# State products interleaved with the gate products, and adaLN sums moved forward and onto VectorE, in a two-layer trunk

## The chip, the core and the metric

One NeuronCore of a Trainium2 chip runs the whole program. The metric is the device time of one execution in microseconds. The kernel before has a median of 759.27 us over 3 runs (758.9 to 759.5).

## The reference, cut to what matters

The trunk has two layers for 256 tokens of width 1024. Layer 0 mixes tokens by gated linear attention (GLA), layer 1 by a recurrent block (RG-LRU); each is followed by a mixture of 16 experts of which every token uses 2. Shifts, scales and gates of all of them ("adaLN vectors") come from one conditioning vector `c` and large matrices `ada_w`. All arithmetic is float32.

```python
cond = silu(c)
for i in range(2):
    sh1, sc1, g1, sh2, sc2, g2 = split(cond @ ada_w[i] + ada_b[i], 6)
    h = rmsnorm(x, norm_mix_g[i]) * (1 + sc1) + sh1
    x = x + g1 * (gla_mixer(h, ...) if i == 0 else lru_mixer(h, ...))
    h = rmsnorm(x, norm_ffn_g[i]) * (1 + sc2) + sh2
    x = x + g2 * grouped_moe(h, ...)
return rmsnorm(x, final_norm_g)
```

In the GLA mixer four chunks of 64 tokens follow each other: the state of a chunk is `S_n = diag(gamma_n) S_{n-1} + k_dec^T v`, for four heads of 128 x 256 each, and its output is `o_n = q_n^T S_n`, normed and multiplied by `silu(g)`; then comes `w_out`.

## The kernel before

**The stream.** Every large weight comes in pieces of 128 x 2048 float32 (1 MB), issued by SyncE in one order that `plan` writes down as a text (lines 285 to 287). `a10` is layer 0's adaLN vector 1, half 0 (two pieces); `A..` the same of layer 1; `i4` two pieces of the mixer's input matrix, `I2` and `J2` one half of one each; `o` the output matrix (four pieces); `u0` to `u6` the units of the expert block. u0 holds the experts 0 and 1 at fixed places, 12 pieces; u1 to u6 hold the others in an order that is known only after the routing (`r_ordi`, line 951, read by SyncE at line 242). The pieces lie in a ring of 17 slots, which also holds the mixer's large tiles (`big`: v, the states S, sg, oT, xg). A piece is issued when a slot is free.

**The adaLN vectors.** `jobs` lists them in the order of the stream. `fill` (line 303) sums one half of a vector on VectorE: one scaling and seven multiply-adds of 128 x 512 (lines 319 and 317), at a low priority, so that they stand where VectorE would otherwise be idle; a gate ("wide") gets a ninth operation (line 321). The others sum into one of two buffers `acc`. `settle` (line 343) finishes what `fill` left: a matmul with ones for a gate (line 349), four transposes (line 353), a reduction (line 356) and one or two small operations for the others. `fill_now` (line 325) does the same sum on TensorE with 16 matmuls (line 338) and a copy by ScalarE.

**The order of work.** The program is written with a scheduler: it orders each engine's instructions by their place in the program (or their priority) and by when it thinks their inputs are ready, and gives out slots and buffers. Only in the output projection (`out_route`, line 463) is TensorE's order that of the text.

**Layer 0's mixer** (`gla`, line 533). The k, v and gate projections use I2, I3, I1, J2, J3, J1; the q projection (line 613) i0. The constants of layer 1's mixer (`lru_consts`, line 704) are worked out in between, in some 25 operations of 128 x 8 on VectorE. The states follow for both tiles of 128 tokens: 16 products per tile (line 629), which VectorE copies into S or adds to the state before (lines 637 and 639). Then the g projection in two halves (i4 and i5, line 529), the outputs `o_part` (line 655), their gating (line 666) and the transposes `turn` (line 674).

**Layer 0's output and routing** (`out_route`). Four parts of `w_out` (line 473), by tile m and half hf, each followed by two VectorE operations that add to x (lines 475 and 476). Between their matmuls stand the transposes of x, the router's products (line 830) and the settlements. `scores` (lines 834 and 835: `r_z`, then a sigmoid on ScalarE), `choose` (lines 843 to 863) and `route_count` pick the experts of one tile; behind the second tile's, `route_order` (lines 941 to 951) sorts the experts by load and writes `r_ordi`. A10 and A11 are filled behind the first tile's `choose`; A00 and A01 are `fill_now`, one ahead of tile 1's routing and one behind its `choose`. What is owed then (a50, a51, A10, A11, A00, A01) is settled in the expert block, between u0's up products (line 1030) and its down products (line 1041).

Of the kernel before, what the change touches and what calls it, by code (L numbers as in the profile page):

```python
# [10 lines left out]
OP = mybir.AluOpType  # L11
# [3 lines left out]
P = 128  # L15
D = 1024
S = 256
NM = S // P
# [57 lines left out]
def trunk(ctx, tc, I, out):  # L76
# [16 lines left out]
    def mid(name):  # L93
        return wk.tile([P, 1024], F32, name="mid", tag="mid", bufs=3)
# [171 lines left out]
    def plan(l, text):  # L266

        for n in text.split():
            if n[0] == "a":
                stream.add("a", *ada_pieces(l, int(n[1]), int(n[2])))  # L270
            elif n[0] == "A":
                stream.add("a", *ada_pieces(1, int(n[1]), int(n[2])))
            elif n[0] == "i":
                w = (gw_in, lw_in)[l]
                stream.add("i", k_piece(w, 0, int(n[1]) * 512), k_piece(w, 1, int(n[1]) * 512))
            elif n[0] in "IJ":
                stream.add("i", k_piece((gw_in, lw_in)[l], "IJ".index(n[0]), int(n[1]) * 512))
            elif n == "r":
                stream.add("r", gate_piece(I["lru_w_r"][0]), gate_piece(I["lru_w_i"][0]))
            elif n == "o":  # L280
                stream.add("o", *[row_piece(I[("gla_w_out", "lru_w_out")[l]][0], q) for q in range(4)])
            else:
                stream.add("u", *moe_pieces(l, UNITS[int(n[1])]))

    plan(0, "a10 a00 I2 a11 I3 a01 I1 J2 J3 J1 i0 a20 a21 i4 a40 a41 i5 a30 a31 a50 a51 o A10 A11 A00 A01 "
            "u0 u1 u2 u3 u4 u5 u6")
    plan(1, "i2 i3 a20 r i0 a21 a40 i1 a41 a30 a31 o a50 a51 u0 u1 u2 u3 u4 u5 u6")

# [51 lines left out]
        A.copy(acc, ps)  # L340
        owed.append((acc, dst[:, 4 * hf:4 * hf + 4], r, gain + hf if gain is not None else None, True))

    def settle(n=99):

        for _ in range(min(n, len(owed))):
            acc, dst, r, gain, four = owed.pop(0)
            ps = bank()
            if dst is None:
                T.matmul(ps, ones, acc, start=True, stop=True)
                A.copy(acc, ps)  # L350
                continue
            for j in range(4):
                T.transpose(ps[:, j * P:(j + 1) * P], acc.rearrange("r (p j) -> r j p", j=4)[:, j, :], ident)

            rows_of = ps.rearrange("p (j q r) -> p j q r", j=4, q=4)[:, :, :, 0] if four else ps.rearrange("p (j q) -> p j q", j=4)
            V.tensor_reduce(dst, rows_of, axis=AX.X, op=OP.add)
            if gain is None:
                V.tensor_tensor(dst, dst, tabT[:, :, r], op=OP.add)
            else:
                V.scalar_tensor_tensor(dst, dst, 1.0, tabT[:, :, r], op0=OP.add, op1=OP.add)  # L360
                V.tensor_mul(dst, dst, tabT[:, :, gain])
# [98 lines left out]
    def out_route(l, yT, gate, gs, rest=None, last=None):  # L460

        w = [stream.get("o").rearrange("p (j n) -> p j n", j=2) for _ in range(4)]
        stream.look = SLOTS - 2
        h, hT = new_h()
        R = route_begin()

        def part(m, hf, between={}):
            sl = slice(hf * 512, (hf + 1) * 512)
            ps = bank()
            for k in range(8):  # L470
                if k in between:
                    between[k]()
                T.matmul(ps, yT[:, k, m * P:(m + 1) * P], w[k // 2][:, k % 2, sl], start=k == 0, stop=k == 7)  # L473
            tmp = s2("tmp")
            V.tensor_mul(tmp, ps, gate[:, sl])
            b = V.tensor_add(x[:, m, sl], x[:, m, sl], tmp)
            mark["x"] = b.ins

        def first():
            turn_h(x, hT, 0, halves=[1])  # L480
            stats_of[0] = stats(0)
            scaled(h, 0, stats_of[0])

        late = len(jobs) > 2
        stats_of = [None, None]
        with tc.manual_schedule(engines={T.engine}):
            part(0, 0)
            part(0, 1, {3: lambda: turn_h(x, hT, 0, halves=[0])})
            if rest:
                rest()  # L490
            router(R, gs)
            part(1, 0, {2: lambda: settle(2), 4: first, 6: lambda: router_shift(R, gs[1], 0), 7: lambda: logits(R, hT, 0)})
            router_shift(R, gs[1], 1)
            scores(R, 0, stats_of[0])
            choose(R, 0)
            fill(2)
            part(1, 1, {3: lambda: turn_h(x, hT, 1, halves=[0]), 5: lambda: logits(R, hT, 1, halves=[0]),
                        7: lambda: route_count(R, 0)})
            stream.ahead(stream.at + SLOTS - 1)
            r = stats(1)  # L500
            if late:
                accs = mid("acc")
                fill_now(accs[:, 0:512])
            else:
                settle(1)
            turn_h(x, hT, 1, halves=[1])
            xg, oh = gather_begin(R)
            gather_tile(R, h, oh, 0, 0, [0])
            logits(R, hT, 1, halves=[1])
            scores(R, 1, r)  # L510
            scaled(h, 1, r)
            gather_tile(R, h, oh, 0, 0, [1, 2, 3])
            choose(R, 1)
            gather_tile(R, h, oh, 0, 1)
            route_count(R, 1)
            if late:
                fill_now(accs[:, 512:1024])
            else:
                settle(1)
            if last:  # L520
                last()
            gather_end(l, R, h, xg, gs)
        R["xg"] = xg
        return h, hT, R
# [11 lines left out]
    def gla(gs):  # L536
# [40 lines left out]
            T.matmul(ps[32 * q:32 * q + 32, 0:S], wa[:, k, :], hT[:, k, :], start=k < 4, stop=k >= 4)  # L577
        V.tensor_scalar(alr, ps[:, 0:S], e16, None, op0=OP.add)
        half_proj(0, 1)
        for m in range(NM):  # L580
            A.copy(v[:, m, 0:512], pst[0][m])

# [5 lines left out]
        for m in range(NM):  # L588
            A.activation(ed[:, m], ed[:, m], AF.Ln, bias=1.0)
            V.scalar_tensor_tensor(la[:, m], psz[m], 0.0, ed[:, m], op0=OP.min, op1=OP.subtract)  # L590
        half_proj(1, 1)
        for m in range(NM):
            A.copy(v[:, m, 512:1024], pst[1][m])
        half_proj(2, 1)
        psg = bank()
        for m in range(NM):
            ps = bank()
# [12 lines left out]
        for hd in range(4):  # L610
# [1 line left out]
            for k in range(8):  # L612
                T.matmul(ps[:, 0:S], w[k // 4][:, k % 4, hd * P:(hd + 1) * P], hT[:, k, :], start=k == 0, stop=k == 7)
            A.activation(qT[:, hd], ps[:, 0:S], AF.Copy, scale=128.0 ** -0.5)
        fill(2)
        k0.extend(lru_consts())


        Sb = [big("S").rearrange("p (c n) -> p c n", c=2) for _ in range(2)]
        St = [Sb[c // 2][:, c % 2].rearrange("p (h n) -> p h n", h=4) for c in range(4)]  # L620

        for m in range(NM):
            for h2 in range(2):
                pair = [bank(), bank()]
                for hh in range(2):
                    hd = 2 * h2 + hh
                    for c in range(2):
                        rows_of = slice(64 * c, 64 * c + 64)
                        T.matmul(pair[c][:, hh * 256:(hh + 1) * 256], kd[rows_of, m, hd * P:(hd + 1) * P],
                                 v[rows_of, m, hd * 256:(hd + 1) * 256], start=True, stop=True)  # L630
                for c in range(2):
                    k = 2 * m + c
                    for hh in range(2):
                        hd = 2 * h2 + hh
                        src = pair[c][:, hh * 256:(hh + 1) * 256]
                        if k == 0:
                            V.tensor_copy(St[k][:, hd], src)  # L637
                        else:
                            V.scalar_tensor_tensor(St[k][:, hd], St[k - 1][:, hd], gam[:, hd * 4 + k:hd * 4 + k + 1],
                                                   src, op0=OP.mult, op1=OP.add)  # L640
        sg = big("sg").rearrange("p (m n) -> p m n", m=2)

        def g_part(hf, m, w):
# [26 lines left out]
        def turn(m, hf):  # L670
# [4 lines left out]
            for b in range(2):  # L675
# [4 lines left out]
                else:  # L680
                    V.tensor_scalar(dst, src, ngT[:, b:b + 1], None, op0=OP.mult)

        w = get2()
        for m in range(NM):
            g_part(0, m, w)
        fill(2)
        os = [o_part(m) for m in range(NM)]
        for m in range(NM):
            gated(m, 0, *os[m])
        settle(2)  # L690
        w = get2()
        g_part(1, 0, w)
        gated(0, 1, *os[0])
# [2 lines left out]
            turn(m, 0)  # L696
        g_part(1, 1, w)
        gated(1, 1, *os[1])
        fill(4)
        settle(2)  # L700
        turn(0, 1)
        return oT[0], lambda: turn(1, 1)

# [108 lines left out]
    def router_shift(R, s, at):  # L812

        ps = R["ps"][:, 3 * NE:4 * NE]
        if at == 0:
            R["b"] = sm.tile([1, NE], F32, name="r_b", bufs=1)
            for k in range(8):
                T.matmul(ps[0:1], s[:, k:k + 1], rw[:, k, :], start=k == 0, stop=k == 7)
            V.tensor_copy(R["b"], ps[0:1])
        else:  # L820
            R["bb"] = rt("bb", NE)
            T.matmul(ps, ones[0:1, :], R["b"], start=True, stop=True)
            V.tensor_copy(R["bb"], ps)
# [425 lines left out]
```

## Time and profile before

| | us |
|---|---|
| median of 3 runs | 759.27 |
| the profiled execution | 757.96 |
| its span, first to last instruction | 756.2 |
| TensorE busy | 699.6 |
| VectorE busy | 340.4 |
| ScalarE busy | 131.4 |
| weights and others moved by DMA | 286.27 MB, 379 GB/s on average |

The page divides the span into 40 slices of 18.9 us. Windows and timelines give stretches in microseconds from the span's start; "PEclk" is the TensorE clock that was granted (1.00 is full speed), "DMA share" the mean busy share of the 16 DMA engines. In a timeline, instructions of one line that follow each other are one row: start, time from the first's start to the last's end, engine, line, operation, operands, count, and in brackets the idle time before it with what ended it. SPq is the queue in which SyncE issues DMAs.

### The profile page before, as it was taken

How to read it: one execution, taken by the hardware profiler on the slowest of the kernel's cores; microseconds unless marked ns; L12 is line 12 of the kernel's file. 1: busy time of each engine (PE TensorE's matmuls, PEld its weight loads, DVE VectorE, ACT ScalarE, POOL GpSimd, SP SyncE). 2: the span in 40 equal slices, each digit the busy share in tenths (PEclk: the TensorE clock that was granted, in tenths of full speed). 3: DMA queues.
4: the chain of work that ended last, by engine and by line, in shares of the span. 5: the costliest groups of instructions: out<-in, count | busy, mean ns of one | idle time of the engine just before them, and what ended most of it. 6: DMA issues, size and time to landing. Idle time of an engine off the chain costs nothing. (4 is left out here: it accounts for less than half of the span.)

```text
span 756.2 us, 9538 instructions
## 1 busy us (share of the span) xinstructions
PE 699.6 (93%) x3559; PEld 342.8 (45%) x3559; DVE 340.4 (45%) x780; ACT 131.4 (17%) x257; POOL 27.4 (4%) x69
## 2 busy tenths in 40 slices
PE   4899899999999999999887999998999999999874
PEld 3345745454633533533226888655433433433212
DVE  3626983897413223231023589996523143140214
ACT  5006112122200000000013166123210010010002
POOL 5000001000000000000000014000000000000000
PEclk9999999999999999999999999999999999999998
DMA  9999999779999999999999999991999999999994
GB/s 304 384 386 387 386 396 386 269 318 384 423 370 422 421 421 420 423 409 422 411 363 379 381 367 350 406 377 59 423 421 419 419 421 421 421 420 410 422 373 150
DMA packets 80445, 286.27 MB, mean 379 GB/s; under 512 B 5991, under 2 KB 16280, under 8 KB 57866
## 3 DMA queue, kind: packets, MB, share of 16 engines
q1 hardware_dynamic: 78752, 284.71, 96.0%
q10 hardware_dynamic: 1258, 0.66, 0.3%
q8 instruction: 30, 0.49, 0.3%
q0 software_dynamic: 384, 0.23, 0.1%
q14 instruction: 21, 0.17, 0.1%
HBM read 284.54 MB, written 1.05 MB: 378 GB/s over the span
## 5 line engine op out<-in xcount | busy, mean ns | idle before, releaser
L1030 PE MATMUL ps<-w 128*32 128x512 f32 (+1 forms) x1280 | 204.1, 593 | 9.6 <-DMA w<-in_moe_w_up_dram 7.4
L1030 PEld LDWEIGHTS ps<-w 128*32 128x32 f32 (+1 forms) x1280 | 61.8, 121 | 148.7 <-issue 121.7
L1041 PE MATMUL ps<-w,s 128*32 128x512 f32 (+1 forms) x512 | 85.0, 594 | 2.7 <-ACT s L1160 2.7
L1147 DVE TENSOR_TENSOR s<-s,ps 128x512 f32<-128x512 f32 x14 | 9.6, 688 | 149.6 <-PE ps L1030 149.6
L1061 DVE TENSOR_TENSOR x<-x,ps 128x512 f32<-128x512 f32 (+1 forms) x60 | 39.1, 652 | 59.7 <-PE ps L1060 59.7
L317 DVE SCALAR_TENSOR_TENSOR acc<-w,cond,acc 128x512 f32<-128x512 f32 x84 | 64.8, 794 | 1.1
L473 PE MATMUL ps<-w 128*128 128x512 f32 x128 | 59.3, 599 | 0.0
L1060 PE MATMUL ps<-mid,s 128*128 128x512 f32 (+1 forms) x120 | 55.1, 581 | 2.9 <-DVE mid L1168 2.6
L740 PE MATMUL ps<-hT,w 128*128 128x256 f32 x256 | 55.7, 379 | 0.0
L1041 PEld LDWEIGHTS ps<-w,s 128*32 128x32 f32 (+1 forms) x512 | 25.6, 123 | 58.3 <-issue 50.9
L740 PEld LDWEIGHTS ps<-hT,w 128*128 128x128 f32 x256 | 48.7, 191 | 6.7 <-ACT hT L423 0.2
L1179 DVE TENSOR_TENSOR mid<-ps,gate 128x512 f32<-128x512 f32 x24 | 16.6, 692 | 64.7 <-PE ps L1041 64.7
L561 PE MATMUL ps<-w,hT 128*128 128x512 f32 x96 | 42.5, 596 | 1.8 <-DVE hT L425 1.0
L904 PE MATMUL ps<-onehot,h 128*128 128x256 f32 x192 | 42.4, 379 | 0.0
L317 DVE SCALAR_TENSOR_TENSOR gate<-w,cond,gate 128x512 f32<-128x512 f32 x56 | 40.9, 748 | 0.9
L1146 ACT ACTIVATE s<-ps 128x512 f32<-128x512 f32 x14 | 8.4, 597 | 183.6 <-PE ps L1030 183.6
L904 PEld LDWEIGHTS ps<-onehot,h 128*128 128x128 f32 x192 | 36.4, 190 | 7.0 <-issue 2.4
L1060 PEld LDWEIGHTS ps<-mid,s 128*128 128x128 f32 x120 | 20.5, 190 | 30.8 <-issue 20.1
L1160 ACT COPY s<-ps 128x512 f32<-128x512 f32 x14 | 8.2, 586 | 147.2 <-PE ps L1158 147.2
L529 PE MATMUL ps<-w,hT 128*128 128x512 f32 x64 | 29.6, 619 | 3.7 <-DVE w L637 3.7
L473 PEld LDWEIGHTS ps<-w 128*128 128x128 f32 x128 | 22.8, 191 | 20.7 <-issue 18.9
L561 PEld LDWEIGHTS ps<-w,hT 128*128 128x128 f32 x96 | 17.8, 190 | 23.9 <-issue 21.0
(261 smaller groups left out, 602.5 us busy)
## 6 DMA issues: line engine op xcount, KB each, us to landing
w<-in_moe_w_gate_dram SPq DMA_DIRECT2D x64, 1024.0 KB, 11.2
w<-in_moe_w_up_dram SPq DMA_DIRECT2D x64, 1024.0 KB, 15.7
w<-in_moe_w_down_dram SPq DMA_DIRECT2D x56, 1024.0 KB, 17.8
w<-in_ada_w_dram SPq DMA_DIRECT2D x48, 1024.0 KB, 13.5
w<-in_gla_w_in_dram SPq DMA_DIRECT2D x12, 1024.0 KB, 14.6
w<-in_moe_w_down_dram SPq DMA_DIRECT2D x16, 512.0 KB, 9.5
w<-in_lru_w_in_dram SPq DMA_DIRECT2D x8, 1024.0 KB, 12.5
w<-in_gla_w_out_dram SPq DMA_DIRECT2D x4, 1024.0 KB, 12.5
```

Source lines behind the costliest of these rows:

```text
L317: V.scalar_tensor_tensor(acc, w, cond[:, k:k + 1], acc, op0=OP.mult, op1=OP.add)
L473: T.matmul(ps, yT[:, k, m * P:(m + 1) * P], w[k // 2][:, k % 2, sl], start=k == 0, stop=k == 7)
L529: T.matmul(ps, hT[:, k, m * P:(m + 1) * P], w[k // 4][:, k % 4, :], start=k == 0, stop=k == 7)
L561: T.matmul(pst[i][m], hT[:, 4 * b + j, m * P:(m + 1) * P], w[:, j], start=b == 0 and j == 0, stop=b == 1 and j == 3)
L740: T.matmul(ps[:, 0:S], w[k // 4][:, k % 4, ct * P:(ct + 1) * P], hT[:, k, :], start=k == 0, stop=k == 7)
L904: T.matmul(ps[j // 2][:, j % 2 * 2 * P:(j % 2 + 1) * 2 * P], hv[:, b, j, :], oh, start=m == 0 and j % 2 == 0, stop=m == 1 and j % 2 == 1, ...
L1030: T.matmul(ps[p0:p0 + n], xg[:, k, t0 + p0:t0 + p0 + n], w[i][:, j, :], start=k == 0, stop=k == 7)
L1041: T.matmul(ps[hf][p0:p0 + n], aT[:, k, p0:p0 + n], w[i][:, j, hf * 512:(hf + 1) * 512], start=k == 0, stop=k == 3)
L1060: T.matmul(ps, wt[:, m * P:(m + 1) * P], y[:, sl], start=True, stop=True)
L1061: V.tensor_add(x[:, m, sl], x[:, m, sl], ps)
L1147: V.tensor_mul(act, act, pu)
L1179: V.tensor_mul(y[:, sl], py[hf], g2[:, sl])
```

## The change

The GLA's state products of a tile are followed at once by that tile's first g product, instead of all state products coming first. The adaLN pieces a20 to a41, a31, a50, a51, A10 and A11 stand nearer the front of the stream, and the calls of `fill` and `settle` move with them, from between the later parts of the mixer to between the earlier ones. In layer 0's output projection `fill_now` is gone: A00 and A01 are summed by `fill` like the others, behind the settlement of A10 and A11, whose buffers they use; a30 and a31 are settled in the mixer, a50 and a51 where `fill_now` stood. Functions that only change their place (`g_part`, `o_part`, `gated`, `turn`) are left out.

```diff
-    plan(0, "a10 a00 I2 a11 I3 a01 I1 J2 J3 J1 i0 a20 a21 i4 a40 a41 i5 a30 a31 a50 a51 o A10 A11 A00 A01 "
+    plan(0, "a10 a00 I2 a11 I3 a01 I1 J2 a20 J3 a21 J1 a40 i0 a41 a30 i4 a31 a50 a51 i5 A10 A11 o A00 A01 "
             "u0 u1 u2 u3 u4 u5 u6")
...
-    def settle(n=99):
-
-        for _ in range(min(n, len(owed))):
-            acc, dst, r, gain, four = owed.pop(0)
+    def settle(n=99, skip=0):
+
+        for _ in range(min(n, len(owed) - skip)):
+            acc, dst, r, gain, four = owed.pop(skip)
...
-        late = len(jobs) > 2
+        late = rest is not None
...
-            part(1, 0, {2: lambda: settle(2), 4: first, 6: lambda: router_shift(R, gs[1], 0), 7: lambda: logits(R, hT, 0)})
+            part(1, 0, {2: lambda: late or settle(2), 4: first, 6: lambda: router_shift(R, gs[1], 0), 7: lambda: logits(R, hT, 0)})
             router_shift(R, gs[1], 1)
             scores(R, 0, stats_of[0])
             choose(R, 0)
+            if late:
+                settle(2, 2)
             fill(2)
             part(1, 1, {3: lambda: turn_h(x, hT, 1, halves=[0]), 5: lambda: logits(R, hT, 1, halves=[0]),
                         7: lambda: route_count(R, 0)})
             stream.ahead(stream.at + SLOTS - 1)
             r = stats(1)
-            if late:
-                accs = mid("acc")
-                fill_now(accs[:, 0:512])
-            else:
-                settle(1)
+            settle(1)
             turn_h(x, hT, 1, halves=[1])
...
             route_count(R, 1)
-            if late:
-                fill_now(accs[:, 512:1024])
-            else:
-                settle(1)
+            settle(1)
...
         half_proj(0, 1)
+        fill()
...
         half_proj(1, 1)
+        fill()
...
         half_proj(2, 1)
+        fill()
...
-        fill(2)
+        fill()
+        settle(3)
+        fill()
         k0.extend(lru_consts())
...
-        for m in range(NM):
+        def states(m):
             for h2 in range(2):
                 pair = [bank(), bank()]
...
         w = get2()
         for m in range(NM):
+            states(m)
             g_part(0, m, w)
-        fill(2)
+        settle(1)
+        fill(3)
         os = [o_part(m) for m in range(NM)]
         for m in range(NM):
             gated(m, 0, *os[m])
-        settle(2)
         w = get2()
...
         g_part(1, 1, w)
         gated(1, 1, *os[1])
-        fill(4)
         settle(2)
+        fill(2)
         turn(0, 1)
```

## Rows read from the trace of the kernel before

**Rows 1.** The page's second part: DMA rate in 40 slices of the span.
```profile
GB/s 304 384 386 387 386 396 386 269 318 384 423 370 422 421 421 420 423 409 422 411 363 379 381 367 350 406 377 59 423 421 419 419 421 421 421 420 410 422 373 150
```
**Rows 2.** Windows, all engines: stretch, length, busy times, PEclk, DMA share, GB/s.
```profile
50.00:110.00 60.00, 56.28 (x196) 33.20 (x194) 45.54 (x93) 17.17 (x26) 0.00 (x0) 0.97 1.05 388
135.00:139.00 4.00, 4.00 (x11) 1.73 (x10) 4.00 (x7) 0.00 (x0) 0.00 (x0) 1.00 0.07 26
139.00:165.00 26.00, 25.92 (x112) 14.29 (x110) 23.07 (x53) 6.33 (x12) 0.56 (x1) 1.00 0.81 300
...
178.00:181.00 3.00, 3.00 (x21) 1.73 (x22) 1.89 (x6) 1.36 (x4) 0.00 (x0) 1.00 0.62 216
181.00:210.00 29.00, 28.32 (x134) 15.06 (x132) 14.08 (x53) 6.30 (x10) 0.00 (x0) 1.00 1.01 419
210.00:213.00 3.00, 3.00 (x16) 1.01 (x14) 0.02 (x1) 0.00 (x0) 0.00 (x0) 1.00 0.60 194
```
**Rows 3.** SyncE's own waits, 135 to 160 and 160 to 185: total, times, longest.
```profile
SPq L255 <- DVE acc L317: 14.8, 4, 8.8
...
SPq L242 <- DVE r_ordi L951: 10.1, 1, 10.1
```
**Rows 4.** Timeline of VectorE: `r_z` of tile 0 and `r_ordi`, layer 0.
```profile
158.94 0.23 DVE L834 SCALAR_TENSOR_TENSOR r_z<-ps,rstd,r_bb 128x16 f32<-128x16 f32 x1
...
177.41 0.16 DVE L951 CAST r_ordi<-r_ordf 1x14 int32<-1x14 f32 x1
```
**Rows 5.** Timeline of SyncE's DMA issues behind the order, layer 0 and layer 1.
```profile
178.61 1.56 SPq L255 DMA_DIRECT2D w<-in_moe_w_gate_dram  x2
...
210.38 4.38 SPq L255 DMA_DIRECT2D w<-in_moe_w_gate_dram  x4
...
527.42 2.69 SPq L255 DMA_DIRECT2D w<-in_moe_w_gate_dram  x4
...
555.74 4.34 SPq L255 DMA_DIRECT2D w<-in_moe_w_gate_dram  x4
```
**Rows 6.** Timeline of TensorE: q products, state products, g products.
```profile
73.37 14.00 PE L613 MATMUL ps<-hT,w 128*128 128x256 f32 x64
...
87.32 3.77 PE L629 MATMUL ps<-w,h 64*128 64x256 f32 x32
94.81 15.51 PE L529 MATMUL ps<-w,hT 128*128 128x512 f32 x32 [3.72 <-DVE w L637]
...
123.42 7.03 PE L529 MATMUL ps<-w,hT 128*128 128x512 f32 x16
```
**Rows 7.** Timeline of VectorE: the first states copied out.
```profile
94.01 0.75 DVE L637 COPY w<-ps 128x256 f32<-128x256 f32 x2
```
**Rows 8.** Window of TensorE behind the hole: busy, PEclk, DMA share, GB/s.
```profile
94.80:98.00 3.20, 3.19 (x4) 0.52 1.05 387
```
**Rows 9.** Windows of VectorE: two of all its work, then one of line 317 alone.
```profile
159.17:177.57 18.40, 16.09 (x68) 1.00 0.94 391
...
119.00:131.00 12.00, 1.70 (x5) 1.00 1.05 385
...
159.17:167.17 8.00, 5.71 (x8) 1.00 0.86 349
```
**Rows 10.** Timeline of VectorE: the first operation of a20.
```profile
55.89 0.49 DVE L319 TENSOR_SCALAR gate<-w,cond 128x512 f32<-128x512 f32 x1 [7.74 <-DMA w<-in_ada_w_dram]
```
**Rows 11.** Timeline of TensorE: the first `fill_now` of the projection, and settlements.
```profile
167.06 1.92 PE L338 MATMUL ps<-w,cond 128*32 128x512 f32 x16
...
194.85 1.88 PE L349 MATMUL ps<-gate,one 128*128 128x512 f32 x4
196.57 1.11 PE L353 MATMUL ps<-ident,acc 128*128 128x128 f32 x8
```
**Rows 12.** Timeline of VectorE: operations of the sums, and two settlements' reductions.
```profile
134.63 4.72 DVE L317 SCALAR_TENSOR_TENSOR acc<-w,cond,acc 128x512 f32<-128x512 f32 x7
...
150.49 1.28 DVE L356 TENSOR_REDUCE sh<-ps 128x4 f32<-128x512 f32 x2
```

More of the change, by code (lines that the diff above doesn't have):

```diff
@@ L620, in gla @@
         St = [Sb[c // 2][:, c % 2].rearrange("p (h n) -> p h n", h=4) for c in range(4)]
-        for m in range(NM):
[L623 to L640, printed above, removed]
         sg = big("sg").rearrange("p (m n) -> p m n", m=2)
@@ L681, in turn @@
                     V.tensor_scalar(dst, src, ngT[:, b:b + 1], None, op0=OP.mult)
+        def states(m):
+            for h2 in range(2):
+                pair = [bank(), bank()]
+                for hh in range(2):
+                    hd = 2 * h2 + hh
+                    for c in range(2):
+                        rows_of = slice(64 * c, 64 * c + 64)
+                        T.matmul(pair[c][:, hh * 256:(hh + 1) * 256], kd[rows_of, m, hd * P:(hd + 1) * P],
+                                 v[rows_of, m, hd * 256:(hd + 1) * 256], start=True, stop=True)
+                for c in range(2):
+                    k = 2 * m + c
+                    for hh in range(2):
+                        hd = 2 * h2 + hh
+                        src = pair[c][:, hh * 256:(hh + 1) * 256]
+                        if k == 0:
+                            V.tensor_copy(St[k][:, hd], src)
+                        else:
+                            V.scalar_tensor_tensor(St[k][:, hd], St[k - 1][:, hd], gam[:, hd * 4 + k:hd * 4 + k + 1],
+                                                   src, op0=OP.mult, op1=OP.add)
         w = get2()
         for m in range(NM):
+            states(m)
             g_part(0, m, w)
-        fill(2)
+        settle(1)
+        fill(3)
         os = [o_part(m) for m in range(NM)]
```

## The prediction

> **What bounds the kernel now.** I read the page's second part first: the DMA rate in 40 slices [rows 1]. It lies near 385 GB/s while layer 0's mixer runs, near 420 in the expert blocks, and falls off in slices 7 and 8 (132 to 170 us) and in slice 27. So the kernel streams weights, and what can be won lies in stretches where the stream stands still before the expert blocks. The windows split the first one [rows 2]: 7% DMA share from 135 to 139 us, 81% from 139 to 165, 62% from 178 to 181, 60% from 210 to 213; in between and after it is 1.01, full.
>
> Which of these gaps sets the end? SyncE's own waits answer [rows 3]. Up to 165 us it waits for ring slots that VectorE's adaLN sums still hold (8.8 us at the longest). Then it waits 10.1 us for `r_ordi`, the order of the routed experts, without which no further weight has an address. VectorE writes it at 177.41 to 177.57 us [rows 4], and the next issue is at 178.61 [rows 5]. At that point everything that may be loaded has been loaded: the share drops to 62%. So the gaps before 165 us cost nothing by themselves. Whatever is loaded sooner only waits longer for the order. The time of `r_ordi` is the one that the end follows, since the stream is full from there to the end of the block but for the gap at 210.
>
> What sets `r_ordi`? TensorE from 87 to 167 us with one hole: the 32 state products end near 91.1, then TensorE stands for 3.72 us for VectorE to copy a state out [rows 6], which starts at 94.01 behind the long chain of tiny `lru_consts` operations [rows 7]. For the first 3 us after the hole the granted clock is 0.52 [rows 8], near the lower level, 1.2 GHz. The two g products behind it take 15.51 us, where a single one later takes 7.03 [rows 6]: 15.51 - 14.06 = 1.45 us lost. From part(1,1) on it is VectorE: of the 18.40 us from the end of `r_z` to `r_ordi` it is busy 16.09 [rows 9].
>
> **The change, step by step, against the profiled execution** (757.96 us, span 756.2; the median of the runs is 759.27, 1.3 above, and the difference found is carried over to it).
>
> 1. *States interleaved.* Between the two tiles' state products now stands one g product of 7.03 us, in which VectorE can copy out the first tile's states. Hole and slow clock both go: -3.72 - 1.45 = -5.2 us on TensorE. Bounds: -5.2 to 0, the latter if VectorE, with `lru_consts` and now a30's sum in the same stretch, still keeps the banks. I take -5.2, since 7 us of cover stand against some 3 us of copies (eight at 0.37, half of the 0.75 that the first two took [rows 7]).
>
> 2. *Stream order.* Behind the 17th piece, whose first use waits for its transfer until 55.89 us [rows 10], a piece of 1.05 MB takes 2.70 us at 388 GB/s [rows 2]. So i0 (now up to the 22nd) lands by 69.4, used at 73.37 [rows 6]; i4 (28th) by 85.6, used near 92; o's last piece (44th) by 128.8, used near 133, as its product starts near 127.6 and needs it at three quarters of 7.03 us. Cost 0; the cover is 4 us or more at each, and a slip beyond it would move TensorE by the excess. SyncE issues the same number of DMAs; no other queue is passed.
>
> 3. *Sums and settlements moved forward.* a20 to a41 were settled before and are now, at other places: 0. Settling a30 and a31 moves from within the output projection to before it: 0 at `r_z`. Two settlements cost 1.11 us [rows 11]. Settling A10 and A11 now stands ahead of part(1,1): +1.1 on TensorE behind `r_z`. The first `fill_now` (1.92 us, 16 matmuls [rows 11]) gives way to one wide settlement, half of 1.88; both lie beside VectorE's residual add, 0. VectorE has room for a30 and a31 earlier: it was busy 1.70 us of 12 from 119 to 131 [rows 9].
>
> 4. *A00 and A01 summed by VectorE.* This is the step that costs. Their accumulators are the buffers of A10 and A11, which come free only once the settlement behind `choose(0)` is through TensorE, that is behind `r_z`. So all 16 operations start in the stretch that ends with `r_ordi`. Consecutive ones start 0.66 us apart (seven in 4.72, the last of them 0.74 long [rows 12], so 0.08 over each other); two scalings at 0.49 [rows 10] - 0.08 = 0.41: 14 x 0.66 + 2 x 0.41 = 10.1 us. Settling A10 and A11 adds two reductions and four small operations, 1.28 + 0.2 = 1.5 us [rows 12]. In exchange, the eight operations of A10 and A11 that fall here now (5.71 us busy [rows 9], 8 x 0.66 = 5.3) have moved ahead. Low priority doesn't keep them off the path: those eight stood among the steps of `choose(0)` too, one wherever a step waited for the step before.
> New busy time: 16.09 - 5.3 + 10.1 + 1.5 = 22.4 us. The old idle of 2.3 (18.40 - 16.09) is between kept and filled; I take half, 1.2. So `r_ordi` comes 23.6 us after `r_z`. With `r_z` 5.2 us earlier (153.97), that is 177.57: **no change at all**. Bounds: -1.2 to +1.1 from the idle time, and 0.66 less for every sum that slips behind `r_ordi`.
> The rows show operations starting 0.08 us before the recorded end of the one before [rows 12]. The Trainium skill (VectorE: DVE Perf Modes, "The DRAIN you can't avoid") says that the next operation does not start until the pipeline has emptied; read as the recorded end, it would price 16 sums at the full 0.74 and 0.48, 1.3 us more, and the order would come that much later. The trace's spacing decides here.
>
> 5. *The gap at 210 us.* After the order, SyncE issues again until all slots are full, and the next issue waits for shared experts' down pieces: 210.38 - 178.61 = 31.8 us after the first routed issue [rows 5]. In layer 1 the same distance is 555.74 - 527.42 = 28.3. Between them stand the settlements of six vectors: 1.88 us wide and twice 1.1 narrow [rows 11]. The change leaves one pair: -3.0 us, so 28.8, near layer 1's distance. The gap held 3 us at 60% against 1.01 [rows 2]: -1.2 us. Bounds 0 and -1.2; I take -1.2.
>
> **Sum:** 0.0 - 1.2 = -1.2 us: 756.8 for the profiled execution, 758.1 for the median. A measurement of this kernel can tell about 0.2%, 1.5 us, from no change.
>
> **Rivals.**
> *A. The sums stay off the path.* If they wait until `r_ordi` is out (VectorE is slack during the first experts' products), the order gains what TensorE does: -5.2 + 1.1 = -4.1, and with step 5 the time is 754.0. Against it: the eight sums in `choose(0)` [rows 9]; and four ring slots would then be held when routed loads want them.
> *B. The wait comes back elsewhere (slower).* `lru_consts` is still ahead of the state copies, and a30's eight operations can go between its steps (8 x 0.66 = 5.3 us). TensorE then waits at tile 1's state products for banks. From 1.2 us of lost gain on, the change loses its gain; with all 5.2 lost, step 4 stays unpaid: +5.2 - 1.2 = +4.0, 763.3. For it: the old hole had this very cause [rows 6, 7]. Against: the 7 us of cover.
> *C. It doesn't do what it says.* The order on TensorE is written out only in the output projection; here a scheduler may still put all states first. Same price, 763.3.
> *D. The idle DMA time is itself the prize.* From 135 to 165 us, 4 x 0.94 + 26 x 0.20 = 9.0 us of full rate are missing [rows 2]; with slots freed sooner they would be filled: 750.3. Against it: the wait for `r_ordi`. The Trainium skill (Perfetto Trace Analysis, "Identifying the Most-Contended Engine") says to optimize the most-contended engine first; by occupancy that is the DMA, and by that rule D would be the result.
>
> **How the numbers follow.** Forecast 0.55 (of it faster 0.21, same 0.32, slower 0.02, as its bounds reach from -3 to +1); A 0.18; D 0.03; B 0.16, of which 0.03 loses little enough to count as same; C 0.08, of which 0.02. Faster 0.42, same 0.37, slower 0.21. The range goes from A's 754.0 to 760.6, half of B: what is left out is D, C and the worse half of B, together under 0.2.
>
> **What would show it.** Right: no hole of TensorE over 1 us between the state products and the second g product, granted clock 1.00 there, `r_z` near 154; sums (line 317) among the steps of `choose(1)`; `r_ordi` within 1.2 us of 177.6; a longer wait for `r_ordi` on SyncE; DMA full 30 us after the first routed issue. Wrong: `r_ordi` near 173.5 (A) or past 180 (B, C), or a first routed issue long after `r_ordi` for want of slots.

## The result, and the profile after

The changed kernel takes 777.71 us (median of 4 runs, 777.51 to 778.16); the kernel before, run beside it, 759.38. The ratio is 1.0235, with a 95% interval from 1.0213 to 1.0257: **slower by 18 us**, where 1.2 us less had been forecast. The profiled execution of the changed kernel took 778.16 us, its span 776.4, at a mean granted clock of 0.969.

The first view is again the page's second part, the DMA rate in 40 slices of the span (19.4 us each):

```profile
GB/s 295 387 386 387 387 387 398 245 234 217 268 398 421 421 421 421 420 422 410 422 385 371 375 386 344 388 420 130 311 421 421 420 421 420 422 420 399 422 376 152
```

The dip that took two slices in [rows 1] now takes four (136 to 213 us); behind it the row looks like the old one. SyncE's own waits from 125 to 205 us (total, times, longest) answer to [rows 3]:

```profile
SPq L255 <- DVE acc L317: 18.9, 5, 6.8
SPq L255 <- PE ps L473: 18.5, 4, 12.6
SPq L242 <- DVE r_ordi L952: 16.5, 1, 16.5
```

The wait for the order has grown from 10.1 to 16.5 us, and the waits for TensorE's output projection are 18.5 us: the stream stands ready and the routing is late. How late, the timeline of VectorE shows, as in [rows 4], and those of SyncE's issues behind the order in both layers, as in [rows 5]:

```profile
171.92 0.23 DVE L835 SCALAR_TENSOR_TENSOR r_z<-ps,rstd,r_bb 128x16 f32<-128x16 f32 x1
...
197.65 0.16 DVE L952 CAST r_ordi<-r_ordf 1x14 int32<-1x14 f32 x1
```

```profile
198.85 2.72 SPq L255 DMA_DIRECT2D w<-in_moe_w_gate_dram  x4
...
230.38 4.64 SPq L255 DMA_DIRECT2D w<-in_moe_w_gate_dram  x4
...
546.63 2.68 SPq L255 DMA_DIRECT2D w<-in_moe_w_gate_dram  x4
```

`r_ordi` comes 20.24 us later than before (197.65 against 177.41), and the profiled execution is 20.20 us longer (the medians differ by 18.3). So nearly all of it happened ahead of the order, as the forecast had it; what follows moved with it. The 20.24 us have two parts: `r_z` is 12.98 us later, and the stretch from its end to the order's end takes 25.66 us instead of 18.40, 7.26 more.

**The first part** is seen on TensorE, in its timeline (the answer to [rows 6]; L353 is the settlement of a40):

```profile
90.11 0.63 PE L353 MATMUL ps<-ident,acc 128*128 128x128 f32 x4
...
90.69 2.04 PE L671 MATMUL ps<-w,h 64*128 64x256 f32 x16
92.66 7.13 PE L524 MATMUL ps<-w,hT 128*128 128x512 f32 x16
99.72 1.99 PE L671 MATMUL ps<-w,h 64*128 64x256 f32 x12
114.78 2.07 PE L671 MATMUL ps<-w,h 64*128 64x256 f32 x4 [13.06 <-DVE w L679]
116.78 9.05 PE L524 MATMUL ps<-w,hT 128*128 128x512 f32 x16
```

The interleaving is there: 16 state products, a g product, then 12 of the other 16. But the last four wait 13.06 us for a bank that VectorE has to empty (line 679), where the old hole was 3.72 us. VectorE's timeline up to that time (`gs` is what the settlement of a40 writes):

```profile
90.78 0.69 DVE L356 TENSOR_REDUCE gs<-ps 128x4 f32<-128x512 f32 x1 [8.77 <-PE ps L353]
...
100.51 0.16 DVE L731 TENSOR_SCALAR sp<-lc_t 128x8 f32<-128x8 f32 x1
100.58 0.48 DVE L319 TENSOR_SCALAR gate<-w,cond 128x512 f32<-128x512 f32 x1
101.10 5.48 DVE L317 SCALAR_TENSOR_TENSOR gate<-w,cond,gate 128x512 f32<-128x512 f32 x7
106.61 0.75 DVE L321 SCALAR_TENSOR_TENSOR gate<-tab,ident,gate 128x512 f32<-128x512 f32 x1
107.28 0.48 DVE L319 TENSOR_SCALAR gate<-w,cond 128x512 f32<-128x512 f32 x1
107.80 5.48 DVE L317 SCALAR_TENSOR_TENSOR gate<-w,cond,gate 128x512 f32<-128x512 f32 x7
113.31 0.75 DVE L321 SCALAR_TENSOR_TENSOR gate<-tab,ident,gate 128x512 f32<-128x512 f32 x1
113.97 0.75 DVE L679 COPY w<-ps 128x256 f32<-128x256 f32 x2
```

`lru_consts` ends at 100.67. Then come the 18 operations that sum a50 and a51, 13.4 us, and only then, at 113.97, the first copy of a state whose product had been done since about 92.7. VectorE keeps to the order that was laid down for it: in e9 below it stands idle for 9.36 us in front of such a sum while the states lie ready. So the low priority of the sums no longer helps once they stand ahead. Windows of all engines (stretch, length, busy times, granted clock, DMA share, GB/s) show what the hole does to TensorE's clock, as [rows 8] did:

```profile
101.70:114.80 13.10, 0.04 (x2) 0.02 (x1) 12.57 (x20) 0.00 (x0) 0.00 (x0) 0.57 1.05 387
114.80:118.00 3.20, 3.20 (x6) 1.84 (x7) 3.20 (x9) 0.00 (x0) 0.00 (x0) 0.50 1.05 397
118.00:126.00 8.00, 8.00 (x19) 3.58 (x18) 2.08 (x6) 0.13 (x1) 0.00 (x0) 0.83 1.03 407
```

Behind the hole TensorE runs at 0.50, the lower level of 1.2 GHz, so the g product takes 9.05 us and not 7.13. The hole and this slowness, 13.06 + 1.92, make 15.0 us.

**The second part**, windows of the stretch from `r_z` to the order: first whole, as the first line of [rows 9], then three windows of its end and what follows it.

```profile
172.15:197.81 25.66, 17.83 (x72) 11.99 (x71) 21.62 (x82) 4.75 (x10) 1.03 (x1) 0.83 0.42 164
```

```profile
185.00:192.00 7.00, 5.09 (x24) 5.12 (x24) 4.94 (x16) 1.43 (x2) 0.78 (x1) 0.54 0.12 48
192.00:197.80 5.80, 2.34 (x10) 1.22 (x10) 5.23 (x26) 0.59 (x1) 0.00 (x0) 0.79 0.00 0
197.80:202.00 4.20, 4.20 (x18) 3.39 (x19) 1.20 (x5) 0.46 (x1) 0.00 (x0) 0.50 0.47 158
```

VectorE's busy time there rose from 16.09 to 21.62 us; TensorE's clock, 1.00 throughout before, falls to 0.54 in the middle of the routing and is 0.50 when the gathers run. TensorE's own waits in the same stretch (total, times, longest) show that it stood still between its turns:

```profile
PE ps L923 <- DVE onehot L898: 4.6, 2, 3.1
PE ps L873 <- DVE r_ohs L864: 1.9, 1, 1.9
PE ps L433 <- DVE x L476: 1.3, 1, 1.3
```

TensorE stands 7.8 us for VectorE, and VectorE in turn 25.66 - 21.62 = 4.0 us, almost all of it for TensorE. The two engines pass the work to and fro, and the sums lengthen VectorE's turns (e2 and e3 below take them out).

### The profile page after: what moved, and what is told of

Same layout as the page of the kernel before. It is cut to its first block, busy times and chain, and to the rows that moved or that the text cites. A ratio compares the mean times of both kernels' runs of the same rounds, so it can differ in the third digit from the quotient of the medians.

```text
span 776.4 us, 9485 instructions
## 1 busy us (share of the span) xinstructions
PE 705.7 (91%) x3527; PEld 349.1 (45%) x3527; DVE 351.5 (45%) x796; ACT 130.6 (17%) x255; POOL 27.4 (4%) x69
## 5 line engine op out<-in xcount | busy, mean ns | idle before, releaser
L1031 PE MATMUL ps<-w 128*32 128x512 f32 (+1 forms) x1280 | 208.1, 604 | 9.6 <-DMA w<-in_moe_w_up_dram 7.7
L1031 PEld LDWEIGHTS ps<-w 128*32 128x32 f32 (+1 forms) x1280 | 63.4, 123 | 151.1 <-issue 124.7
L317 DVE SCALAR_TENSOR_TENSOR acc<-w,cond,acc 128x512 f32<-128x512 f32 x98 | 75.6, 789 | 1.3
L556 PE MATMUL ps<-w,hT 128*128 128x512 f32 x96 | 43.9, 614 | 1.0 <-issue 1.0
L524 PE MATMUL ps<-w,hT 128*128 128x512 f32 x64 | 30.3, 630 | 0.0
L556 PEld LDWEIGHTS ps<-w,hT 128*128 128x128 f32 x96 | 18.5, 196 | 23.8 <-issue 22.0
## 6 DMA issues: line engine op xcount, KB each, us to landing
w<-in_gla_w_out_dram SPq DMA_DIRECT2D x4, 1024.0 KB, 13.4
```

The lines of the kernel that those rows point to most:

```text
L317: V.scalar_tensor_tensor(acc, w, cond[:, k:k + 1], acc, op0=OP.mult, op1=OP.add)
L524: T.matmul(ps, hT[:, k, m * P:(m + 1) * P], w[k // 4][:, k % 4, :], start=k == 0, stop=k == 7)
L556: T.matmul(pst[i][m], hT[:, 4 * b + j, m * P:(m + 1) * P], w[:, j], start=b == 0 and j == 0, stop=b == 1 and j == 3)
L1031: T.matmul(ps[p0:p0 + n], xg[:, k, t0 + p0:t0 + p0 + n], w[i][:, j, :], start=k == 0, stop=k == 7)
```

## The experiments

Nine kernels, each against the kernel before on the same chip (its medians lay from 759.3 to 759.8 us).

### The two parts of the loss, apart and together

The first idea was that two separate costs add up: the sums of a50 and a51 ahead of the state copies, and the sums of A00 and A01 ahead of the order. Four kernels make this a table.

**e1: the sums of a31, a50 and a51 held behind the last state operation.**

```diff
-                            V.scalar_tensor_tensor(St[k][:, hd], St[k - 1][:, hd], gam[...],
-                                                   src, op0=OP.mult, op1=OP.add)
+                            b = V.scalar_tensor_tensor(St[k][:, hd], St[k - 1][:, hd], gam[...],
+                                                       src, op0=OP.mult, op1=OP.add)
+                            mark["states"] = b.ins
...
-        fill(3)
+        with tc.issue_after(mark["states"]):
+            fill(3)
```

> The changed kernel, but the sums of a31, a50 and a51 are held behind the last state copy on VectorE. Theory (two separate costs): the 13.06 us hole of TensorE is there because the 18 operations of a50 and a51 stand ahead of the state copies on VectorE, and the sums of A00 and A01 cost another 7.3 us between r_z and r_ordi. Then the hole shrinks to under 1.5 us, r_z comes some 14 us earlier (near 158), r_z to r_ordi stays at 24 to 26 us, and the time is 761 to 764. Rival R1 (one cost): the longer stretch behind r_z only comes of the late and slow TensorE; then r_z to r_ordi falls back to 18 to 19 us and the time is 755 to 758. Rival R2 (ring slots): the state copies need a slot that only the sums of a50 and a51 free; then VectorE waits at the first copy, a hole of 10 us or more stays, and the time is 775 or more.

Measured: 762.76 us (6 runs), ratio 1.0041, interval 1.0028 to 1.0054. TensorE's timeline has no hole (all 16 state products of the second tile stand in one row, 2.79 us long), and the stretch from `r_z` (156.07) to the order stays as long as in the changed kernel:

```profile
100.03 2.79 PE L671 MATMUL ps<-w,h 64*128 64x256 f32 x16
```

```profile
156.30:182.38 26.08, 19.19 (x72) 12.60 (x71) 21.63 (x82) 4.75 (x10) 1.03 (x1) 0.74 0.49 190
```

**e2: A00 and A01 back on TensorE by `fill_now`**, all else as changed.

```diff
             if late:
                 settle(2, 2)
-            fill(2)
+            else:
+                fill(2)
...
-            settle(1)
+            if late:
+                accs = mid("acc")
+                fill_now(accs[:, 0:512])
+            else:
+                settle(1)
```

(and likewise for the second half, behind `route_count(R, 1)`.)

> The changed kernel, but A00 and A01 are summed by TensorE again, as before the change; the sums of a50 and a51 stay where they are. Theory (two costs): the hole stays at 13 us, r_z to r_ordi falls from 25.7 to about 19 us (2 us of it the settlement of A10 and A11), and the time is 769 to 772. R1 (one cost, the hole): r_z to r_ordi stays above 23 us and the time stays at 776 to 778. R2 says the same as the theory here.

Measured: 771.43 us (4 runs), ratio 1.0148, interval 1.0129 to 1.0167. The hole of 13.06 us is there, `r_z` at 172.91, but the stretch behind it is 19.22 us, and the clock in it 1.00:

```profile
173.14:192.36 19.22, 17.13 (x101) 9.78 (x100) 12.84 (x65) 4.66 (x10) 0.56 (x1) 1.00 0.59 220
```

**e3: both edits.**

> Both edits: sums of a31, a50, a51 behind the state copies, and A00 and A01 on TensorE. Theory (two costs): no hole over 1.5 us, r_z near 155, r_ordi 173 to 176, time 753 to 757, below the kernel before. R1: the same as the first kernel of this call, 755 to 758. R2: the hole stays, 768 or more.

Measured: 755.14 us (4 runs), ratio 0.9946, interval 0.9925 to 0.9967: faster than before. The stretch, in the same columns:

```profile
156.12:175.34 19.22, 17.14 (x101) 9.78 (x100) 12.83 (x65) 4.64 (x10) 0.56 (x1) 1.00 0.69 257
```

**e4: the kernel before with the interleaving alone.**

```diff
-        for m in range(NM):
+        def states(m):
             for h2 in range(2):
...
         for m in range(NM):
+            states(m)
             g_part(0, m, w)
```

> The kernel before, with one thing changed: the state products of a tile are followed by its first g product. Stream, sums and settlements are those of before. If the prediction's first step is right by itself (hole of 3.72 us and 1.45 us of slow clock both gone, -5.2 us, and the order and the end follow TensorE), r_ordi comes near 172.3 and the time is 753.5 to 755. If VectorE's chain of small operations still keeps the banks, 1 to 3 us of a hole stay and the time is 755.5 to 758. If the end does not follow the order, the time stays within 1 us of 759.4.

Measured: 754.45 us (4 runs), ratio 0.9932, interval 0.9912 to 0.9952. TensorE's timeline is the one that had been forecast for the change:

```profile
87.42 2.05 PE L629 MATMUL ps<-w,h 64*128 64x256 f32 x16
89.39 7.13 PE L529 MATMUL ps<-w,hT 128*128 128x512 f32 x16
96.46 2.10 PE L629 MATMUL ps<-w,h 64*128 64x256 f32 x16
```

The times of e1 to e3 lie in the ranges of the theory of two costs, and e4's in that of step 1; one cost (R1) fell by e1 and e2, ring slots (R2) by e1. What follows: the hole costs 14.95 us (777.71 - 762.76) with the sums of A00 and A01 on VectorE and 16.29 (771.43 - 755.14) without; these sums cost 6.28 us (777.71 - 771.43) with the hole and 7.62 (762.76 - 755.14) without. The two add up within 1.4 us, about what a measurement can tell, so they are separate costs. And with both taken out, the rest of the change beyond the interleaving (the stream's order, the moved settlements) is worth nothing that shows in the time: 755.14 against e4's 754.45, with overlapping intervals. In the profiled executions two things nearly cancel there: e3's order is out 2.5 us later than e4's (175.34 against 172.86), and its span ends 576.4 us behind the order, e4's 579.5.

### What puts the sums ahead of the state copies

e1 shows that it is their place on VectorE that costs. Three kernels ask what put them there, without ordering anything by hand.

**e6: a50 and a51 behind i5 in the stream, taken and summed behind the last g product**, where the kernel before had them.

```diff
-    plan(0, "... i4 a31 a50 a51 i5 A10 A11 o A00 A01 "
+    plan(0, "... i4 a31 i5 a50 a51 A10 A11 o A00 A01 "
...
-        fill(3)
+        fill(1)
...
         settle(2)
-        fill(2)
+        fill(4)
         turn(0, 1)
```

> Edit: the changed kernel, with a50 and a51 behind i5 again in the stream, and taken and summed behind the last g product, where the kernel before had them; a31's sum stays ahead of the output products, no wait is ordered by hand. Theory (it is the place in the program of a50's and a51's sums, ahead of the state copies of tile 1 in readiness, that lets them go ahead of the copies; a31's sum can't go ahead as it waits for an accumulator that TensorE frees only behind the hole): the copies start near 92 to 96 us, no hole of TensorE over 2 us before the second states, r_z at 155 to 158, and the time 760 to 764.5, as e1 with its explicit hold (762.8). Rival (the early a41 and a30 ahead of the copies are enough: 8 or more sums between the steps of lru_consts, then the copies behind them): a hole of 5 to 8 us stays, time 767 to 772. Rival (the stream's order, not the sums, made the hole): 776 to 779.

Measured: 777.29 us (4 runs), ratio 1.0248, interval 1.0221 to 1.0275. The same 18 operations stand ahead of the copies (from 99.70 us), and the hole is 13.26 us:

```profile
113.90 2.07 PE L671 MATMUL ps<-w,h 64*128 64x256 f32 x4 [13.26 <-DVE w L679]
```

**The theory fell**: their place in the program isn't what lets them ahead. The number was that of the rival which put it on the stream's order, and not on the sums; e1, which keeps that order and has no hole, had already told against this rival as it was worded.

**e7: the interleaving undone**, all else as changed.

```diff
         for m in range(NM):
             states(m)
+        for m in range(NM):
             g_part(0, m, w)
```

> Edit: the changed kernel with its interleaving undone: all 32 state products first, then the two g products, as in the kernel before; the rest of the change stays. Theory (the new stream order and the early sums put a50's and a51's 18 operations ahead of the state copies, whatever TensorE's order is, and interleaving is worth one g product of cover, 7 us): the copies start near 114 us as in the changed kernel, TensorE stands for 18 to 21 us between the last state product and the first g product instead of 13.06, r_z at 176 to 180, and the time 782 to 787. Rival (interleaving itself changed VectorE's order): the copies come behind lru_consts, near 101 us, the hole is 6 to 9 us, and the time 763 to 770.

Measured: 783.78 us (4 runs), ratio 1.0307, interval 1.0292 to 1.0323, as the theory had it. TensorE's timeline behind the 32 state products (the view ends behind 28 of the 32 g matmuls):

```profile
115.17 15.23 PE L524 MATMUL ps<-w,hT 128*128 128x512 f32 x28 [20.32 <-DVE w L679]
```

The hole is 20.32 us, one g product longer than 13.06. So interleaving didn't bring the sums forward; it hid 7 us of the wait.

**e9: the pieces of a50 and a51 six places later**, behind i5 and the four of `o`.

```diff
-    plan(0, "... i4 a31 a50 a51 i5 A10 A11 o A00 A01 "
+    plan(0, "... i4 a31 i5 o a50 a51 A10 A11 A00 A01 "
...
         stream.look = SLOTS - 2
+        if rest:
+            fill(4)
...
-        fill(3)
+        fill(1)
...
-        fill(2)
         turn(0, 1)
```

> Edit: the changed kernel, with the pieces of a50 and a51 behind i5 and the output projection's four in the stream, six places (some 16 us of transfers) later; their sums and those of A10 and A11 are taken at the start of the output projection. No wait is ordered by hand. Theory (VectorE's order takes a sum ahead of the state copies when its piece is expected to have come by then, whatever stands where in the program): only a few of the 18 operations still go ahead of the copies, for six of them 4 us, so the hole of TensorE ahead of the last states shrinks from 13.06 us to 3 to 6 us, r_z comes at 160 to 166, and the time is 765 to 771, between e1's 762.8 and the changed kernel's 777.7. Rival (the early settlement of a40 ahead of the states, or the sums of a41 and a30, made the order): the hole stays at 12 us or more and the time at 776 to 779. Rival (any delay of the pieces is enough): no hole over 2 us, time 761 to 764.

Measured: 778.83 us (4 runs), ratio 1.0259, interval 1.0242 to 1.0276. Time and hole are in the first rival's ranges and not in the theory's. VectorE's timeline behind `lru_consts`:

```profile
109.99 0.49 DVE L319 TENSOR_SCALAR gate<-w,cond 128x512 f32<-128x512 f32 x1 [9.36 <-DMA w<-in_ada_w_dram]
110.51 3.90 DVE L317 SCALAR_TENSOR_TENSOR gate<-w,cond,gate 128x512 f32<-128x512 f32 x5
114.33 0.75 DVE L681 COPY w<-ps 128x256 f32<-128x256 f32 x2
```

Of the 18 operations only six still stand ahead of the copies, as the theory said. But the first of them waits 9.36 us for its piece, and the finished states wait with it: the hole is 13.46 us. What had been left out of the expectation is that an operation laid down too early costs not its length but the time until its input is there. So the number of operations ahead does change with the pieces' place in the stream (18, or 6).

But that place is not the whole cause. In the kernel before, a50 and a51 stand at the same place of the stream as in e6 (its 33rd to 36th piece), are taken at the same place of the program, and are summed from about the same time on, and yet behind the copies, which run from 94.01 [rows 7] to 100.12:

```profile
100.03 0.48 DVE L319 TENSOR_SCALAR gate<-w,cond 128x512 f32<-128x512 f32 x1
```

One thing that differs is when `lru_consts` is done, which stands ahead of the copies: near 94 us there, at 99.6 in e6 and 100.7 in the changed kernel. In these two VectorE first waits 8.77 us for the settlement of a40, and a30's eight operations go between the steps. So the first rival of e9 (the early settlement of a40, or the early sums) is still standing: no run put that settlement or a30's sum back alone. That the sums ahead of the copies make the hole is shown by e1; what puts them there stays open, and by what reckoning a sum is taken for ready ahead of a state copy isn't seen in any trace.

### What sets the stretch from `r_z` to the order

**e5: as e1, and A00 and A01 taken from the ring and summed only once the order is written.**

```diff
             if late:
                 settle(2, 2)
-            fill(2)
+            else:
+                fill(2)
...
             gather_end(l, R, h, xg, gs)
+        if late:
+            with tc.issue_after(mark["order"]):
+                fill(2)
...
-        V.tensor_copy(ordi, ordf[0:1])
+        b = V.tensor_copy(ordi, ordf[0:1])
+        mark["order"] = b.ins
```

> Edit: as e1_sums_behind_states, and besides the two pieces of A00 and A01 are taken from the ring, and summed by VectorE, only once the order of the routed experts is written. Theory (every sum of these two that VectorE does between the end of r_z and the order delays the order by its own length): r_z near 156, as in e1; the stretch from r_z to r_ordi falls from 26.2 us by the 16 sums, 10.1 us, to 15 to 17 us, so r_ordi at 171 to 173.5, and the time 751 to 754.5, nearly all of the 10 us showing in the time. Rival (four more ring slots are held when routed loads want them): r_ordi as above, but after the first routed issue the next wait comes about 20 us later instead of 30.8, the DMA share falls under 0.9 there, and the time stays near 757 to 761. Rival (TensorE sets this stretch too, since it has two settlements and the gathers in it): r_ordi at 175 or later, time 755 or more.

Measured: 759.03 us (10 runs), ratio 0.9992, interval 0.9982 to 1.0003. The stretch, and VectorE's longest wait in it:

```profile
155.74:175.19 19.45, 15.48 (x72) 9.62 (x71) 12.75 (x67) 4.66 (x10) 0.56 (x1) 0.97 0.70 262
```

```profile
DVE r_ov L889 <- PE ps L876: 4.2, 1, 4.2
```

The theory was half right, and both rivals had a share. The order comes 6.6 us sooner behind `r_z` (19.45 against 26.08), not 10.1: with no sums in its way VectorE waits 4.2 us for TensorE's first count of the routing, which stands behind part(1,1). In e2 and e3, where TensorE does these sums, VectorE waits the same 4.2 us and the stretch is 19.22; in e4 eight sums of A10 and A11 stand in it, and it is 18.39 all the same. So some 18 to 19 us remain for the chain through both engines, of which TensorE is busy 15.5 to 17.1; no run took that chain apart. And the slots are missed. SyncE's timeline, and its waits from 165 to 190 us:

```profile
181.29 5.83 SPq L255 DMA_DIRECT2D w<-in_moe_w_gate_dram  x4
```

```profile
SPq L255 <- DVE bc L967: 5.3, 1, 5.3
```

The order is out at 175.19 and the first routed issue comes at 181.29, 6.1 us later, where the other kernels take 1.0 to 1.1: 5.3 us of it is a wait for a slot (the instruction that the row names ended about then; which holder gave up the slot isn't settled). Of the 7.2 us that the order gains on e1, the issue gains 2.2. So the rival's price (757 to 761 us) was right, but the slots are missed ahead of the first routed issue and not behind it: the next wait comes 208.45 - 181.29 = 27.2 us later and not 20.

### The settlements behind the order

**e8: e4, and the two wide settlements (a50, a51) moved ahead of TensorE's last count.**

```diff
             gather_tile(R, h, oh, 0, 1)
+            if late:
+                settle(2)
             route_count(R, 1)
```

> Edit: the kernel before with the interleaving alone (e4_interleave_alone), and the two wide settlements (a50, a51) moved from behind the order to ahead of TensorE's last count of the routing. Theory (TensorE sets the stretch from r_z to r_ordi at 18.4 us in this version, with only 0.9 us of waiting ahead of that count): the order comes 0.7 to 1.3 us later behind r_z than in e4 (19.1 to 19.8 us), the next wait of SyncE comes 29.9 us behind the first routed issue instead of 31.8, and the two cancel but for a few tenths: time 753.5 to 755.5. Rival (VectorE alone sets that stretch): the order stays 18.5 us behind r_z and the time is 752 to 753.5. Rival of step 5 (the distance from the first routed issue to the next wait isn't TensorE's work): the distance stays at 31.5 to 32 us and the time is 755 to 757.

Measured: 753.09 us (5 runs), ratio 0.9911, interval 0.9897 to 0.9924. The time lies in the range of the first rival (752 to 753.5), just under the theory's. The stretch is 18.94 us (e4: 18.39), between the theory's 19.1 and that rival's 18.5: with 1.9 us more on TensorE the order comes 0.55 us later behind `r_z`. The next wait comes 205.27 - 175.22 = 30.05 us behind the first routed issue, as the theory said (e4: 31.76). Windows of the gap, first of e4, then of e8:

```profile
205.00:208.00 3.00, 3.00 (x16) 1.01 (x14) 0.00 (x0) 0.00 (x0) 0.00 (x0) 1.00 0.71 197
```

```profile
205.00:208.00 3.00, 3.00 (x16) 1.00 (x14) 0.13 (x1) 0.00 (x0) 0.00 (x0) 1.00 1.03 426
```

The gap is closed. e8 beats both the kernel before (by 6.7 us) and the changed one; whether it beats e4 isn't settled, as their intervals overlap.

## Why the prediction was wrong, point by point

**What bounds the kernel** held: the time follows `r_ordi`. The span ends 578.6 us behind the order before and after the change, and 576.4 to 579.5 behind it in all other kernels but e5 (582.8), where slots were missing.

**Step 1 is the step that failed.** It took -5.2 us, "since 7 us of cover stand against some 3 us of copies", with 0 as its other bound. The wait that it had wrong is TensorE's wait for the copies: their length was weighed against the cover, and not what might stand ahead of them on VectorE. There stood 18 operations of 13.4 us. The hole costs 15 to 16 us against the same kernel without it (e1, e3), and `r_z` came 13 us later than before and not 5 earlier. Interleaving itself was sized rightly: alone it gave 4.85 us (e4), and in the changed kernel some 6 (e7). What undid it belongs to step 3, which priced the earlier sums of a30 and a31 at nothing, since VectorE had room, and did not look at those of a50 and a51, nor ask where in VectorE's order they would land. It also took the settlement of a40 at 0 at its new place, where VectorE waits 8.77 us for it; whether that brought the sums ahead isn't shown.

**Rival B** named the mechanism (TensorE waits at tile 1's state products for banks) and let only a30's eight operations go between the steps of `lru_consts`. They did, from 91.59 to 97.67, and `lru_consts` ended at 100.67; but a50's and a51's followed. Its worst case of +5.2 us was the old hole come back, and nothing said that a new hole could be no longer than the old one.

**Step 4** had the sign and the mechanism: all 16 sums stand between `r_z` and the order. Busy time was forecast at 22.4 us and came to 21.62. The term that was mis-sized is the idle time: 1.2 us ("I take half") against 4.0. VectorE's waits for TensorE are not slack that sums fill; where they push TensorE's work back, the wait comes again at the next exchange, and TensorE comes back at a lower clock. The stretch was 25.66 us against 23.6. Its credit of 5.3 us for moving A10 and A11 out doesn't show where A00 and A01 are not VectorE's: the stretch is 18.39 us with these eight in e4, and 19.22 without them, but with the settlement of A10 and A11, in e3. What it is worth beside the 16 sums no run shows.

**Step 2** stands: TensorE waits for no transfer from 55 to 135 us, and e3, with the new stream order, is level with e4 in time. **Step 3** put the moved settlements and early sums at 0 ahead of `r_z`; in e3 `r_z` is 1.65 us later than in e4 (155.89 against 154.24), and what of the rest of the change costs it isn't shown.

**Step 5** had the mechanism and left a term out. The distance from the first routed issue to the next wait was to be 28.8 us and was 31.53. Both wide settlements had left it, and one narrow pair. But the gathers behind the order, and the start of u0's up products, run at the lower clock (0.50 from 197.8 to 202 us). TensorE's timeline, before and after:

```profile
177.17 2.05 PE L922 MATMUL ps<-onehot,h 128*128 128x128 f32 x16 [0.63 <-DVE onehot L897]
179.15 13.95 PE L1030 MATMUL ps<-w 128*64 128x512 f32 x64
```

```profile
197.40 3.79 PE L923 MATMUL ps<-onehot,h 128*128 128x128 f32 x16 [1.52 <-DVE onehot L898]
201.12 14.66 PE L1031 MATMUL ps<-w 128*64 128x512 f32 x64
```

The up products start 2.27 us behind the first routed issue instead of 0.54 and take 0.71 longer: 2.4 us of what the settlements gave back are lost again. That the settlements set it is shown by e8: 1.88 us moved away, 1.71 us shorter, and the gap closed, worth 1.4 us by the medians (with overlapping intervals) where 1.2 had been taken.

**Rival A**'s gain in the order is real but smaller (`r_ordi` at 175.03 in e5, not 173.5), and its objection decided: the slots. **Rival C** fell, as TensorE does interleave. **Rival D** fell: the DMA idles more than before, at shares of 0.12 and 0.00 from 185 to 197.8 us, and what it waits for is the order, not slots. The rule of the Trainium skill that was cited for it (Perfetto Trace Analysis, "Identifying the Most-Contended Engine") is to optimize the most contended engine first. For the DMA that section goes by HBM utilization and not by the occupancy that the forecast took. The rule names the engine; that freeing slots would help it was the forecast's reading, which this trace doesn't bear out.

**What would show it:** `r_ordi` past 180 was named there as the sign of B or C, and the profile after has it (197.65), with a hole and a late `r_z` where none were to be seen.

## What to carry to other kernels

Low priority is a rule for whoever lays down the order, not for the engine: once a cheap-looking operation stood ahead of the copy that frees a bank, TensorE waited for all of it (13.06 us), and for its input too (e9). So when work is made available sooner, ask which of the engine's urgent operations it could be put ahead of, and tie it behind them by an explicit order, as e1 did. And where two engines hand work to each other, as in this routing, idle time of one need not be room for more work: 5.5 us more of VectorE's work made the stretch 7.3 us longer.

## What the runs showed of the hardware that was not expected

The same multiply-add of 128 x 512 has two spacings. In the changed kernel's hole seven of them follow each other into one sum, in 5.48 us with 0.75 for the last: one starts (5.48 - 0.75) / 6 = 0.79 us after another, later than the one before has ended. In [rows 12] seven take 4.72 us, 0.66 apart. In e4 both spacings stand in one place on VectorE:

```profile
101.28 1.54 DVE L317 SCALAR_TENSOR_TENSOR gate<-w,cond,gate 128x512 f32<-128x512 f32 x2
...
105.16 4.72 DVE L317 SCALAR_TENSOR_TENSOR gate<-w,cond,gate 128x512 f32<-128x512 f32 x7
```

The first two belong to one half (1.54 - 0.75 = 0.79). Of that half five are left when the second half begins (at 104.76), and the seven stand 0.66 us apart. The likely reading is that they alternate between the two halves, so that none needs the result of the one just before; the views leave out which half an operation belongs to, so this is argued and not shown. The forecast had used 0.66 throughout. For a vector of 16 operations the difference is an estimated 2 us, by these rows. No run changed this alone.
